# Unused columns that move the operand tiles of TensorE to other offsets within 512 bytes

## The chip, the core and the metric

The kernel runs on one core of one Trainium2 chip. Its time is the device time of one launch in microseconds (us): 2973.36 us, the median of three runs (2969.99 to 2975.42). The execution that was profiled took 2971.34 us.

## The reference

Two token streams of 256 tokens each and width 1024, a context (columns 0 to 255 of every tile below) and a latent one (columns 256 to 511), go through four layers. Every layer has a token mixer and then a SwiGLU feed-forward network (FFN); both read an RMSNorm of the stream that is scaled and shifted by vectors made from `c` or `c_ctx`. Layers 0 and 3 mix with a bidirectional state-space scan (SSD), layer 1 with a gated MLP (gMLP), layer 2 with bidirectional retention. The last layer computes the latent stream alone.

```
for i in range(4):
    x = x + g1 * mixer[i % 3](modulate(rmsnorm(x, norm1_g[i]), sh1, sc1))        # latent reads context through scan states
    x = x + g2 * (silu(h @ ffn_w1[i]) * (h @ ffn_w3[i])) @ ffn_w2[i]             # h = modulate(rmsnorm(x, norm2_g[i]), sh2, sc2)
    (the context stream likewise, with its own shifts, scales and gates, except in the last layer)
return rmsnorm(x, final_g)
```

Nearly all of the arithmetic is in the dense products with the weights: `ssd_w_in`, `ssd_w_out`, `gmlp_w_in`, `gmlp_w_out`, `ret_w_in`, `ret_w_out`, and the FFN's three, 1024 by 2816 and back.

## The kernel before

Everything is held with the features on the 128 partitions and the tokens along the free axis. A product of float32 accuracy is made of three float32r products: a matrix is split into a high part (rounded to float32r) and a low part (what the rounding left), and high times high, high times low and low times high are added up in PSUM (`mm3`, L302 to L308). So each pair of 128x128 weight block and activation block gives three matmuls, each with a load of its own for its 128x128 stationary operand:

```
            pe.matmul(pt, lh, rh, start=(start and i == 0), stop=False)
            pe.matmul(pt, lh, rl, start=False, stop=False)
            pe.matmul(pt, ll, rh, start=False, stop=(stop and i == n - 1))
```

The first two arguments behind `pt` are the stationary operand and the moving one; the trace prints the moving one first (`mm<-AH,whi`: `AH` moves, `whi` is stationary). L306 is the first of the three, L307 the second, L308 the third. There are 4,304 of each.

The weights stream in through `emit_dma` and `emit_split`: 512 KB units on SyncE's queue into three staging tiles `st`, split by ScalarE into `whi` (L226) and by VectorE, every fourth time GpSimd, into `wlo` (L227), four buffers of each. Splitting runs three units ahead of the product that uses them.

The moving operands are: `AH`/`AL`, the split normed stream (`proj`, used by all input products); `yg` (from `ytiles`), the split gated output of the mixers and the last four inner tiles of each FFN; in the gMLP for every other block `yh`/`yl`; in the FFN `hh`/`hl` (made by `pair`, two inner tiles of 512 tokens in each, six buffers of each), which `oblock` multiplies with `ffn_w2`. In `wide_job` (gMLP and retention values) it is the other way around: the weights move and `AH`/`AL` are stationary. With both streams a moving operand is 512 columns of float32 (2,048 bytes in each partition), in the last layer and where a stage is started stream by stream it is 256.

Where stages meet, splits that are ahead are put into tiles of the next stage that are free until then (`place`): `hh`/`hl` of the FFN, `V` of the gMLP, `dcc`/`dcl` of the retention, `C2`/`px` of the SSD. They then are stationary operands under those names.

The order of the instructions on each engine is the order in which the program is written out (`tc.manual_schedule`): lists of jobs and slots, with the number of splits ahead as the only rule. Tiles come from pools. A pool takes the next free bytes of a partition's row; a tile is placed behind the one that was first asked for before it, rounded up to 32 bytes, and tiles with a `tag` share `bufs` buffers. The constants' pool `cp` lies first, from byte 16,512 (after the scratch and four constants); `X`, `AH` and `AL` are its first three tiles. `MHALF`, 4 columns with the exponent -0.5 for the norms, stands behind them; after it come `SEL`, `CC`, `IDB`, `NEG0`, `NEG1` and the `yg` tiles, then the pools `wp` (`st`, `whi`, `wlo`) and `sp`, and last the pool of the running stage (`ssd`, `gml`, `ret`, `ffn`, `mod`).

Of the kernel before, what the change touches and what calls it, by code (L numbers as in the profile page):

```python
# [9 lines left out]
F32 = mybir.dt.float32  # L10
F32R = mybir.dt.float32r
# [5 lines left out]
P = 128  # L17
# [3 lines left out]
NTOK = 2 * T  # L21
# [7 lines left out]
FFN_START = (0, 6, 12, 18)  # L29
STOP = DEPTH  # L30
POOL_SHARE = 4


_PRM = {}
# [77 lines left out]
def backbone(ctx, tc, A, out):  # L112
# [3 lines left out]
    cp = ctx.enter_context(tc.tile_pool(name="cp", bufs=1))  # L116
# [6 lines left out]
    def nm(s):  # L123
        serial[0] += 1
        return f"{s}_{serial[0]}"
# [3 lines left out]
    def psum_open(ph, **split):  # L129

        assert sum(split.values()) == 8
        banks["pool"] = ph.enter_context(tc.tile_pool(name=nm("pp"), bufs=1, space=PSUM))
        banks["split"] = split
        banks["cycle"] = [0, ["mm"]]
# [4 lines left out]
    def psm():  # L139
        c = banks["cycle"]  # L140
        c[0] += 1
        return ps(c[1][c[0] % len(c[1])])
# [4 lines left out]
    def f32(ap):  # L147
        return ap.bitcast(F32)
# [6 lines left out]
    CST = cp.tile([P, NCST], F32, name="CST")  # L155
    MOD = cp.tile([P, DEPTH, 2, 48], F32, name="MOD")
    GP = cp.tile([P, DEPTH, 2, 2, 8], F32, name="GP")
    MHALF = cp.tile([P, 4], F32, name="MHALF")
    SEL = cp.tile([P, 64], F32R, name="SEL")
    CC = cp.tile([P, KT, 32], F32, name="CC")  # L160
    BF = mybir.dt.bfloat16
# [22 lines left out]
    lent = set()  # L184
    share = [POOL_SHARE]
    hold = [False]
# [115 lines left out]
    def mm3(pt, pairs, start=True, stop=True):  # L302

        n = len(pairs)
        for i, (lh, ll, rh, rl) in enumerate(pairs):
# [3 lines that stand above are left out]
# [10 lines left out]
    def mjob(unit, evac, n0=0, n1=NTOK):  # L319
        def q(W):  # L320
            evac(proj(W[0], n0, n1), n0, n1)
        return Job([unit], [(q, [0], [0])])

    def mjob_skew(units, evacs, ranges, whole=True):


        quanta = []
        n0, n1 = ranges[0][0], ranges[-1][1]
        pts = {}

        def half(j, a, b, h):
            def f(W):
                if j not in pts:
                    pts[j] = psm()[:, :n1 - n0]
                hi, lo = W[j]
                mm3(pts[j][:, a - n0:b - n0], [
                    (hi[:, k * P:(k + 1) * P], lo[:, k * P:(k + 1) * P], AH[:, k, a:b], AL[:, k, a:b])
                    for k in range(4 * h, 4 * h + 4)], start=(h == 0), stop=(h == 1))
                if h == 1 and not whole:
                    evacs[j](pts.pop(j)[:, a - n0:b - n0], a, b)  # L340
                elif h == 1 and b == n1:
                    evacs[j](pts[j], n0, n1)
            return f
        for a, b in ranges:
            for j in range(0, len(units), 2):
                for h in range(2):
                    for jj in range(j, min(j + 2, len(units))):
                        quanta.append((half(jj, a, b, h), [jj], [jj] if h == 1 and b == n1 else []))
        return Job(units, quanta)
# [122 lines left out]
    def rms_steps(acc, n0, n1, dim, sink):  # L472
# [5 lines left out]
        def s0():  # L478
# [8 lines left out]
            dve.tensor_scalar(ms[:, :nch], pt[:, :nch], 1.0 / dim, EPS, op0=MUL, op1=ADD)  # L487
            pool.tensor_tensor(st["rs"][:, :nch], ms[:, :nch], MHALF[:, :nch], op=POW)

# [84 lines left out]
    def ytiles():  # L574

        return [[cp.tile([P, NTOK], F32R, tag=f"y{a}{k}", name=nm("yg"), bufs=1) for k in range(4)]
                for a in "hl"]


    def resid(i, w, norm):  # L580
        def f(pt, m, n0, n1, last):
            for a, b in split_ranges(n0, n1):
                g = MOD[:, i, vec(a), 24 * w + 16 + m:24 * w + 16 + m + 1]
                dve.scalar_tensor_tensor(  # L584
                    X[:, m, a:b], pt[:, a - n0:b - n0], g, X[:, m, a:b], op0=MUL, op1=ADD)
                if last and (a in norm):
                    norm[a].add(m, dve if m >= 5 + (i < 3 or w == 1) and a == T else pool)
        return f
# [29 lines left out]
    def boundary(last, norms, nxt, ranges, hooks=None, lend=(), pool_share=1):  # L618
# [39 lines left out]
        for k, q in enumerate(open_job(nxt) if nxt is not None else []):  # L658
# [7 lines left out]
            if k == 7:  # L666
                share[0] = POOL_SHARE
        share[0] = POOL_SHARE
        banks["cycle"][1] = ["mm"]
# [558 lines left out]
    def gmlp(i, j, need_ctx, prev_last, prev_ranges, norms, fin_norms):  # L1228
        UN, VN, WOUT = Src("gmlp_u", j), Src("gmlp_v", j), Src("gmlp_out", j)
        with ExitStack() as ph:  # L1230
# [24 lines left out]
            def vnorm():  # L1255
                t = qt([4], "vn")
                dve.tensor_reduce(t, SS, axis=mybir.AxisListType.X, op=ADD)
                dve.tensor_scalar(t, t, 1.0 / 2048.0, EPS, op0=MUL, op1=ADD)
                pool.tensor_tensor(RS, t, MHALF, op=POW)

# [258 lines left out]
    def ffn(i, need_ctx, prev_last, prev_ranges, norms, fin_norms):  # L1519
        W1, W3, W2A, W2B = Src("ffn_w1", i), Src("ffn_w3", i), Src("ffn_w2a", i), Src("ffn_w2b", i)  # L1520
        yr = BOTH if need_ctx else LAT
        n0, n1 = yr[0][0], NTOK
        with ExitStack() as ph:
            q = ph.enter_context(tc.tile_pool(name=nm("ffn"), bufs=1))
            psum_open(ph, mm=7, s=1)
            H = {}
            S1 = {}

            def e1(ct):
                def f(pt, a, b):  # L1530
                    t = q.tile([P, NTOK], F32, tag="s1", name=nm("s1"), bufs=2)
                    act.activation(t[:, :b - a], pt, AF.Silu)  # L1532
                    S1[ct, a] = t
                return f

            def pair():
                return [q.tile([P, 2, NTOK], F32R, tag=t, name=nm(t), bufs=6) for t in ("hh", "hl")]

            def place():
                return [t.rearrange("p a b -> p (a b)") for t in pair()]  # L1540

            def e3(ct):
                def f(pt, a, b):
                    s = S1.pop((ct, a))[:, :b - a]
                    dve.tensor_tensor(s, s, pt, op=MUL)  # L1545
                    if ct == 18 and ct not in H:
                        yt = ytiles()
                        for k in range(4):
                            H[18 + k] = (yt[0][k], yt[1][k])
                    elif ct not in H:  # L1550
                        hh, hl = pair()
                        for k in range(2):
                            H[ct + k] = (hh[:, k], hl[:, k])
                    hh, hl = H[ct]
                    act.copy(hh[:, a:b], s)  # L1555
                    dve.tensor_tensor(hl[:, a:b], s, f32(hh[:, a:b]), op=SUB)
                return f

            def hid(ct):
                return [mjob(W1[ct], e1(ct), n0, n1), mjob(W3[ct], e3(ct), n0, n1)]  # L1560

            ev = resid(i, 1, fin_norms)

            def oblock(kb):
                nk, k0 = FFN_BLOCKS[kb], FFN_START[kb]

                def lazy(m):
                    def q_(W):
                        hi, lo = W[0]
                        pt = psm()[:, :n1 - n0]  # L1570
                        mm3(pt, [(hi[:, k * P:(k + 1) * P], lo[:, k * P:(k + 1) * P],
                                  H[k0 + k][0][:, n0:n1], H[k0 + k][1][:, n0:n1]) for k in range(nk)])
                        ev(pt, m, n0, n1, False)
                    return Job([W2A[kb, m]], [(q_, [0], [0])], 0.75)
                return [lazy(m) for m in range(KT)]

            first_job = mjob_skew([W1[0], W3[0], W1[1], W3[1]], [e1(0), e3(0), e1(1), e3(1)], yr)
            boundary(prev_last, norms, first_job, prev_ranges,
                     lend=[place, place] if need_ctx else [], pool_share=1 if 0 < i < 3 else 2)
            if i == 0 or i + 1 < STOP:  # L1580
                mod_open(ph)
            bg = mod_steps(i + 1, 0, 48) if i + 1 < STOP else []
            seq = []
            for ct in range(2, 12):
                seq += hid(ct)
            seq += oblock(0)
            for ct in range(12, 18):
                seq += hid(ct)
            seq += oblock(1)
            for ct in range(18, 22):  # L1590
                seq += hid(ct)
            seq += oblock(2)
            if i == 0:

                bg = mod_steps(0, 40, 48) + bg
                if STOP == 1:
                    run(seq[:16], bg)
                    seq, bg = seq[16:], []
            run(seq, bg, tail=0)

            k0 = FFN_START[3]
            last = out_last([W2B[mp_] for mp_ in range(4)],
                            lambda: [[H[k0 + k][a] for k in range(4)] for a in range(2)], ev, yr)
            return last, yr
# [8 lines left out]
    act.activation(CC, CC, AF.Silu)  # L1613
    pool.memset(MHALF, -0.5)

# [243 lines left out]
```

## Time and profile before

| | |
|---|---|
| median of three runs | 2973.36 us |
| the profiled execution | 2971.34 us, of which 2969.5 us from its first to its last instruction (the span) |
| TensorE matmul busy | 96% of the span, 16,132 matmuls |
| TensorE weight load busy | 81% |
| VectorE, ScalarE, GpSimd busy | 65%, 37%, 18% |
| DMA engines | 376.37 MB, mean 127 GB/s |
| mean granted TensorE clock | 0.987 of full speed |

PE is TensorE's matmul, PEld its weight load, DVE VectorE, ACT ScalarE, POOL GpSimd. Matmuls are pipelined: the duration of one (0.40 us for 512 columns) overlaps that of the next, so what a matmul costs in a stream is the distance from its start to the start of the next. The timeline view gives the starts: over a run of matmuls that follow each other without a wait, the last start less the first, over the number of steps, is the cost of one.

### The profile page before, as it was taken

How to read it: one execution, taken by the hardware profiler on the slowest of the kernel's cores; microseconds unless marked ns; L12 is line 12 of the kernel's file. 1: busy time of each engine (PE TensorE's matmuls, PEld its weight loads, DVE VectorE, ACT ScalarE, POOL GpSimd, SP SyncE). 2: the span in 40 equal slices, each digit the busy share in tenths (PEclk: the TensorE clock that was granted, in tenths of full speed). 3: DMA queues.
4: the chain of work that ended last, by engine and by line, in shares of the span. 5: the costliest groups of instructions: out<-in, count | busy, mean ns of one | idle time of the engine just before them, and what ended most of it. 6: DMA issues, size and time to landing. Idle time of an engine off the chain costs nothing. (4 is left out here: it accounts for less than half of the span.)

```text
span 2969.5 us, 40647 instructions
## 1 busy us (share of the span) xinstructions
PE 2863.9 (96%) x16132; PEld 2394.7 (81%) x16132; DVE 1923.8 (65%) x3049; ACT 1097.2 (37%) x1934; POOL 529.1 (18%) x405
## 2 busy tenths in 40 slices
PE   7999999899999999999999999999999999999898
PEld 4777777788889878888888777778888888888898
DVE  5776767687875165577776334346777778787644
ACT  4455444322224422422224322234222245544443
POOL 1211112211112100211112111112111142112222
PEclk9999999899999999999999999999999999999899
DMA  6222233255553222355443222223554422223454
GB/s 232 101 86 100 86 107 114 91 189 196 186 183 107 92 78 92 105 183 176 169 169 114 71 74 82 80 77 109 184 183 170 163 86 93 84 87 111 142 178 140
DMA packets 111678, 376.37 MB, mean 127 GB/s; under 512 B 12160, under 2 KB 16640, under 8 KB 111488
## 3 DMA queue, kind: packets, MB, share of 16 engines
q1 hardware_dynamic: 109296, 367.23, 35.6%
q0 software_dynamic: 1616, 5.77, 0.6%
q8 instruction: 127, 2.08, 0.3%
q10 hardware_dynamic: 576, 0.77, 0.1%
q14 instruction: 63, 0.52, 0.1%
HBM read 369.53 MB, written 4.19 MB: 126 GB/s over the span
## 5 line engine op out<-in xcount | busy, mean ns | idle before, releaser
L306 PE MATMUL mm<-AH,whi 128*128 128x512 f32 (+1 forms) x2456 | 897.3, 365 | 4.4 <-DVE xs L823 1.6
L307 PE MATMUL mm<-AL,whi 128*128 128x512 f32 (+1 forms) x2456 | 887.9, 362 | 0.0
L308 PE MATMUL mm<-AH,wlo 128*128 128x512 f32 (+1 forms) x2456 | 886.8, 361 | 0.0
L226 ACT CAST whi<-st 128x1024 fp32r<-128x1024 f32 (+1 forms) x502 | 504.0, 1007 | 362.0 <-PE mm L307 223.8
L227 DVE TENSOR_TENSOR wlo<-st,whi 128x1024 fp32r<-128x1024 f32 (+1 forms) x372 | 448.6, 1210 | 263.5 <-ACT whi L226 263.2
L227 POOL TENSOR_TENSOR wlo<-st,whi 128x1024 fp32r<-128x1024 f32 (+1 forms) x130 | 325.8, 2506 | 1524.9 <-ACT whi L226 1520.3
L306 PEld LDWEIGHTS mm<-AH,whi 128*128 128x128 f32 x2456 | 465.0, 189 | 88.1 <-issue 7.1
L308 PEld LDWEIGHTS mm<-AH,wlo 128*128 128x128 f32 x2456 | 464.6, 189 | 77.8
L307 PEld LDWEIGHTS mm<-AL,whi 128*128 128x128 f32 x2456 | 464.8, 189 | 77.1 <-issue 1.2
L412 DVE SCALAR_TENSOR_TENSOR mj<-mst,cb 128x1024 bf16<-128x1024 f32 x304 | 440.9, 1450 | 34.4 <-DMA mst<-in_mod_w_dram 28.4
L584 DVE SCALAR_TENSOR_TENSOR X<-mm,MOD,X 128x256 f32<-128x256 f32 x332 | 148.1, 478 | 145.8 <-PE mm L308 145.2
L306 PE MATMUL mm<-yg,whi 128*128 128x256 f32 (+1 forms) x592 | 200.2, 338 | 18.7 <-DVE X L584 5.3
L308 PE MATMUL mm<-hh,wlo 128*128 128x512 f32 (+1 forms) x576 | 210.9, 366 | 0.0
L307 PE MATMUL mm<-hl,whi 128*128 128x512 f32 (+1 forms) x576 | 210.8, 366 | 0.0
L306 PE MATMUL mm<-hh,whi 128*128 128x512 f32 (+1 forms) x576 | 210.8, 366 | 0.0
L307 PE MATMUL mm<-yg,whi 128*128 128x256 f32 (+1 forms) x592 | 192.6, 325 | 1.3 <-DVE yg L1089 1.0
L308 PE MATMUL mm<-yg,wlo 128*128 128x256 f32 (+1 forms) x592 | 192.4, 325 | 0.0
L1555 ACT CAST hh<-s 128x512 fp32r<-128x512 f32 (+1 forms) x72 | 40.9, 567 | 297.6 <-DVE s L1545 297.6
L1545 DVE TENSOR_TENSOR s<-s,mm 128x512 f32<-128x512 f32 (+1 forms) x88 | 54.6, 620 | 147.3 <-PE mm L308 147.3
L306 PEld LDWEIGHTS mm<-yg,whi 128*128 128x128 f32 x592 | 113.4, 191 | 33.6 <-DVE X L1133 5.4
L1532 ACT ACTIVATE s<-mm 128x512 f32<-128x512 f32 (+1 forms) x88 | 47.9, 544 | 216.6 <-PE mm L308 216.5
L307 PEld LDWEIGHTS mm<-hl,whi 128*128 128x128 f32 x576 | 108.3, 188 | 19.8
(362 smaller groups left out, 4056.8 us busy)
## 6 DMA issues: line engine op xcount, KB each, us to landing
st<-in_ffn_w_dram SPq DMA_DIRECT2D x176, 512.0 KB, 3.3
mst<-in_mod_w_dram SPq DMA_DIRECT2D x152, 512.0 KB, 4.2
st<-in_ssd_in_dram SPq DMA_DIRECT2D x82, 512.0 KB, 3.3
st<-in_ffn_w2a_dram SPq DMA_DIRECT2D x96, 384.0 KB, 3.0
st<-in_ssd_out_dram SPq DMA_DIRECT2D x32, 512.0 KB, 3.3
st<-in_ret_in_dram SPq DMA_DIRECT2D x32, 512.0 KB, 3.3
st<-in_mod_n_dram SPq DMA_DIRECT2D x24, 512.0 KB, 4.0
st<-in_ffn_w2b_dram SPq DMA_DIRECT2D x16, 512.0 KB, 3.3
```

Source lines behind the costliest of these rows:

```text
L226: act.copy(hi[:, :n], t[:, :n])
L227: (pool if i % share[0] == 0 else dve).tensor_tensor(lo[:, :n], t[:, :n], f32(hi[:, :n]), op=SUB)
L306: pe.matmul(pt, lh, rh, start=(start and i == 0), stop=False)
L307: pe.matmul(pt, lh, rl, start=False, stop=False)
L308: pe.matmul(pt, ll, rh, start=False, stop=(stop and i == n - 1))
L412: dve.scalar_tensor_tensor(j, t, 1.0, mp[1][:, v], op0=MUL, op1=MUL, accum_out=MOD[:, i, v, ct:ct + 1])
L584: dve.scalar_tensor_tensor(X[:, m, a:b], pt[:, a - n0:b - n0], g, X[:, m, a:b], op0=MUL, op1=ADD)
L1532: act.activation(t[:, :b - a], pt, AF.Silu)
L1545: dve.tensor_tensor(s, s, pt, op=MUL)
L1555: act.copy(hh[:, a:b], s)
```

## The change

Three pieces of never-read columns are put in. `MHALF` is asked for with 28 columns in place of 4, and its first four are used: what lies behind it moves by 96 bytes. In each FFN, the first time that `pair` makes its two tiles, a pad of 48 columns (192 bytes) is put before the first `hh` and one of 32 columns (128 bytes) between the `hh` and the `hl` buffers.

```
+PAD_W, PAD_H = 24, (48, 32)
...
-    MHALF = cp.tile([P, 4], F32, name="MHALF")
+    MHALF = cp.tile([P, 4 + PAD_W], F32, name="MHALF")[:, :4]
...
+            pads = []
...
             def pair():
-                return [q.tile([P, 2, NTOK], F32R, tag=t, name=nm(t), bufs=6) for t in ("hh", "hl")]
+                r = []
+                for t, n in zip(("hh", "hl"), PAD_H):
+                    if len(pads) < 2:
+                        pads.append(q.tile([P, n], F32, name=nm("pad")))
+                    r.append(q.tile([P, 2, NTOK], F32R, tag=t, name=nm(t), bufs=6))
+                return r
```

The instructions and their order on every engine stay the same; what changes is where tiles lie. Every tile of the table is a multiple of 512 bytes long, and so are the blocks that the products take out of it, so that a tile has one offset within 512 bytes, whichever buffer and block is used:

| tile | offset modulo 512 before | after |
|---|---|---|
| `X`, `AH`, `AL` | 128 | 128 |
| `st`, `whi`, `wlo`, `yg` | 480 | 64 |
| `hh` | 160 | 448 |
| `hl` | 160 | 64 |
| `V` of the gMLP | 256 | 352 |
| `yh`, `yl` of the gMLP | 288 | 384 |
| `dcc`, `dcl` of the retention | 192 | 288 |
| `C2`, `px`, `E` and the rest of the SSD's large tiles | 480 | 64 |

From this follows, for each kind of product, the distance from the stationary operand's offset to the moving one's (moving less stationary, modulo 512):

| moving / stationary | columns | distance before | after |
|---|---|---|---|
| `AH`, `AL` / `whi`, `wlo` | 512 and 256 | 160 | 64 |
| `hh` / `whi`, `wlo` | 512 and 256 | 192 | 384 |
| `hl` / `whi` | 512 and 256 | 192 | 0 |
| `yg` / `whi`, `wlo` | 512 and 256 | 0 | 0 |
| `yh`, `yl` / `whi`, `wlo` | 512 | 320 | 320 |
| `whi`, `wlo` / `AH`, `AL` | 512 | 352 | 448 |
| `AH`, `AL` / `hh`, `hl` | 256 | 480 | 192, 64 |
| `AH`, `AL` / `dcc`, `dcl` | 256 | 448 | 352 |

## Rows read from the trace of the kernel before

**Rows 1.** The page, busy time and share of the span by engine.
```profile
PE 2863.9 (96%) x16132; PEld 2394.7 (81%) x16132; DVE 1923.8 (65%) x3049; ACT 1097.2 (37%) x1934; POOL 529.1 (18%) x405
```

**Rows 2.** Busy us by stretch (windows): PE, PEld, DVE, ACT, POOL; clock, DMA.
```profile
1190.00:1570.00 380.00, 377.00 (x1803) 311.45 (x1804) 271.84 (x400) 112.09 (x156) 61.25 (x39) 1.00 0.46 161
2384.00:2722.00 338.00, 318.14 (x2419) 287.21 (x2419) 269.73 (x477) 169.18 (x362) 86.64 (x92) 0.98 0.25 88
```

**Rows 3.** Groups by line and shape, xcount, busy us, mean ns, idle before.
```profile
L306 PE MATMUL mm<-AH,whi 128*128 128x512 f32 x1696 | 679.5, 401 | 1.6 <-DVE xs L823 1.6
...
L306 PE MATMUL mm<-AH,whi 128*128 128x256 f32 x760 | 217.8, 287 | 2.7 <-ACT AH L566 1.1 <-DVE GP L442 1.0 <-DVE X L1133 0.6
...
L306 PE MATMUL mm<-hh,whi 128*128 128x512 f32 x432 | 170.6, 395 | 0.0
...
L306 PE MATMUL mm<-whi,AH 128*128 128x512 f32 x256 | 101.9, 398 | 0.0
```

**Rows 4.** Timeline, PE, `AH`/`AL` by weights, 512 columns: start us, us.
```profile
601.77 0.40 PE L308 MATMUL mm<-AH,wlo 128*128 128x512 f32 x1
...
625.91 0.39 PE L306 MATMUL mm<-AH,whi 128*128 128x512 f32 x1
```

**Rows 5.** Timeline, PE, `hh`/`hl` by weights, 512 columns.
```profile
783.19 0.39 PE L306 MATMUL mm<-hh,whi 128*128 128x512 f32 x1
...
803.95 0.39 PE L308 MATMUL mm<-hh,wlo 128*128 128x512 f32 x1
```

**Rows 6.** Timeline, PE, `yg` by weights, 512 columns.
```profile
1128.49 0.39 PE L307 MATMUL mm<-yg,whi 128*128 128x512 f32 x1
...
1135.29 0.39 PE L307 MATMUL mm<-yg,whi 128*128 128x512 f32 x1
```

**Rows 7.** Timeline, PE, gMLP `yh`/`yl` by weights, 512 columns.
```profile
1081.18 0.39 PE L307 MATMUL mm<-yl,whi 128*128 128x512 f32 x1
...
1087.36 0.39 PE L307 MATMUL mm<-yl,whi 128*128 128x512 f32 x1
```

**Rows 8.** Timeline, PE, weights by `AH`/`AL` (`wide_job`), 512 columns.
```profile
970.82 0.39 PE L308 MATMUL mm<-whi,AL 128*128 128x512 f32 x1
...
998.82 0.39 PE L308 MATMUL mm<-whi,AL 128*128 128x512 f32 x1
```

**Rows 9.** Timeline, PE, 256 columns, `AH`/`AL` by weights, last FFN.
```profile
2799.78 0.28 PE L308 MATMUL mm<-AH,wlo 128*128 128x256 f32 x1
...
2814.92 0.28 PE L308 MATMUL mm<-AH,wlo 128*128 128x256 f32 x1
```

**Rows 10.** Timeline, PE, 256 columns, `hh`/`hl` by weights, last FFN, first block.
```profile
2836.74 0.28 PE L308 MATMUL mm<-hh,wlo 128*128 128x256 f32 x1
...
2849.94 0.28 PE L306 MATMUL mm<-hh,whi 128*128 128x256 f32 x1
```

**Rows 11.** Timeline, PE, 256 columns, `hh`/`hl` by weights, last FFN, third block.
```profile
2929.75 0.28 PE L308 MATMUL mm<-hh,wlo 128*128 128x256 f32 x1
...
2941.99 0.28 PE L308 MATMUL mm<-hh,wlo 128*128 128x256 f32 x1
```

**Rows 12.** Timeline, PE, 256 columns, `AH`/`AL` by `dcc`/`dcl`, start of the retention.
```profile
1594.28 0.28 PE L306 MATMUL g<-AH,dcc 128*128 128x256 f32 x1
...
1596.66 0.28 PE L306 MATMUL g<-AH,dcl 128*128 128x256 f32 x1
```

**Rows 13.** Timeline, PE, 256 columns, the same operands, next pair of jobs.
```profile
1599.78 0.28 PE L307 MATMUL g<-AL,dcc 128*128 128x256 f32 x1
...
1600.96 0.28 PE L308 MATMUL g<-AH,dcl 128*128 128x256 f32 x1
```

**Rows 14.** Timeline, PE, 256 columns, `yg` by weights.
```profile
1191.08 0.28 PE L306 MATMUL mm<-yg,whi 128*128 128x256 f32 x1
...
1204.15 0.28 PE L307 MATMUL mm<-yg,whi 128*128 128x256 f32 x1
```

**Rows 15.** Groups by line and shape: the weight load of the first product.
```profile
L306 PEld LDWEIGHTS mm<-AH,whi 128*128 128x128 f32 x2456 | 465.0, 189 | 88.1 <-issue 7.1 <-ACT whi L226 2.2 <-ACT AH L566 1.8
```

## Prediction

> **What bounds the kernel.** I read the page's busy shares first: PE is busy for 2863.9 of 2969.5 us, 96%, and the next engine, DVE, for 65% [rows 1]. Then the busy time by stretch, since a mean over stages can hide one with another limit: in the second FFN PE works 377.0 of 380 us and DVE 271.8, and even in the last SSD, the stage with the most small work, PE has 318 of 338 us against 270 for DVE and 169 for ACT [rows 2]; the granted clock there is 1.00 and 0.98, the level of 2.4 GHz nearly throughout. So PE sets the pace in every stage, and a matmul that gets cheaper or dearer moves the end almost one for one. Last I read the timeline, because the groups' mean durations (0.40 us for 512 columns) overlap and don't give the cost of a matmul. Its starts do: in long runs without a wait, cost is the distance from start to start.
>
> These distances are the core of the case, since all runs below have the same three instructions and the same number of columns:
>
> - `AH`/`AL` by weights, 512 columns, operands 160 bytes apart: 103 steps in 625.91 - 601.77 = 24.14 us, 234.4 ns each [rows 4].
> - `hh`/`hl` by weights, 192 apart: 89 steps in 20.76 us, 233.3 ns [rows 5].
> - weights by `AH`/`AL`, 352 apart: 120 steps in 28.00 us, 233.3 ns [rows 8].
> - `yh`/`yl` by weights, 320 apart: 27 steps in 6.18 us, 228.9 ns [rows 7].
> - `yg` by weights, 0 apart: 30 steps in 6.80 us, 226.7 ns [rows 6].
>
> 512 columns at 2.4 GHz are 213.3 ns, so each pays 13 to 21 ns on top. With 256 columns (106.7 ns): `AH` by weights 129 steps in 15.14 us, 117.4 ns [rows 9]; `yg` 109 steps in 13.07 us, 119.9 ns [rows 14]; `hh` 117.9 ns in one block (112 steps, 13.20 us) [rows 10] and 113.3 ns in a later one on the same buffers and offsets (108 steps, 12.24 us) [rows 11]; `AH` by `dcc`/`dcl` 113.3 ns (21 steps, 2.38 us) [rows 12] and 118.0 ns (10 steps, 1.18 us) [rows 13]. Buffers, PSUM banks and blocks change all along these runs and the distance does not; what differs between the groups is which tiles are read, and so their offsets.
>
> Here a rule speaks against the change. The Trainium skill, "SBUF — State Buffer", section "Who interferes with whom", says that TensorE has one read port for the moving operand and another for LDWEIGHTS, independent of each other, and never waits for anyone. By it the offsets could not matter and the sum of this change would be zero; the 7.7 ns between [rows 4] and [rows 6] are not explained by it.
>
> **What the change does, part by part.** No instruction is added, removed or moved on any engine or queue, and no wait. The pads cost bytes of SBUF alone. What changes is the distance between the two operands that TensorE reads at once: the load of the next stationary operand takes 189 ns [rows 15] and so lies beside the running matmul.
>
> *`AH`/`AL` by weights, 160 to 64.* L306 has 1,696 such matmuls with 512 columns [rows 3], times three lines 5,088. No row has a distance of 64. Two pairs of rows tell which is its nearest: distances 192 (`hh`) and 448 (`dcc`), 256 apart, show the same two values with 256 columns, about 118 and 113.3 ns [rows 10 to 13], while their neighbours show others. I read this as a pattern that repeats after 256 bytes; then 64 is like 320, which is `yh` with 228.9 ns [rows 7]. From 234.4 to 228.9 is 5.5 ns, times 5,088 makes 28.0 us saved. Bounds: at best the 226.7 ns of `yg`, 7.7 ns, 39.2 us saved; on the other side nothing measured lies above 234.4, so I allow as much above it as the best row lies below: 39.2 us lost.
>
> *`hh`/`hl` by weights, 192 to 384 and 0.* 3 x 432 = 1,296 matmuls with 512 columns [rows 3]. A third of them, with `hl`, goes to distance 0: 226.7 ns. For 384 no row with 512 columns exists; between the extremes 226.7 and 234.4 I take the middle, 230.5. The mean (2 x 230.5 + 226.7) / 3 = 229.3 is 4.0 ns under the 233.3 of now: 5.2 us saved. Bounds 8.6 us saved (all at 226.7), 8.6 lost by the same mirror.
>
> *Weights by `AH`/`AL`, 352 to 448.* 3 x 256 = 768 matmuls [rows 3]. If the pattern repeats after 256, 448 is like 192, 233.3 ns as now [rows 5, 8]: 0. Bounds 5.1 us saved or lost (6.6 ns each).
>
> *256 columns.* `AH` by weights, 3 x 760 = 2,280 [rows 3], 160 to 64: rows span 113.3 to 119.9 around 117.4 [rows 9 to 14], and one pair of offsets takes two values, so I take 0, bounds 9.3 us saved (4.1 ns), 9.3 lost.
>
> *What stays:* `yg` and `yh`/`yl` keep their distances, 0 and 320: nothing. The float32 products, DVE, ACT, POOL and the DMAs read and write the same lengths: nothing.
>
> Sum: 28.0 + 5.2 = 33.2 us less. Bounds: all savings 39.2 + 8.6 + 5.1 + 9.3 = 62 us, all losses the same. What could take a gain back is another engine: in the second FFN 380 us would become some 372, with DVE's 272 still far below [rows 2]; ACT and POOL have more room. So I let all of it through. The profiled execution took 2971.34 us, 2.0 under the median of three, 2973.36; against the median the forecast is 2973.4 - 33.2 = 2940 us.
>
> **Rivals.**
>
> *1. The distance 64 is worse (slower).* The place is the 5,088 matmuls of `AH`. The weight load and the moving read both run up their rows while a matmul lasts, and at 64 bytes one may keep meeting the other for longer than at 160. Its price goes up to the mirror bound, 39.2 us on `AH` less the 5.2 of `hh`: 3007 us; with half of the price, 19.6 - 5.2 = 14.4 us, it is 2988. It decides once the step of `AH` is over 235.4 ns (1 ns more is 5.1 us, what `hh` gives). For it: five distances give no smooth curve, so a sixth can lie anywhere. Against: `AH` is already the slowest of the five.
>
> *2. Offsets don't matter (no change).* The difference between [rows 4] and [rows 6] would come from where tiles lie in the large, or from what is stored, and moving them by 96 bytes leaves the steps as they are: 2973 us, within 3. For it: two values for the same offsets [rows 10, 11], which an offset alone can't explain. Against: with 512 columns each kind keeps its step in every buffer, `hh` and `hl` over twelve buffers across 49 KB. This is the result that the Trainium skill's page "SBUF — State Buffer" leads to.
>
> *3. All kinds reach the best row (much faster).* 64, 384 and 448 are all as good as 0, and 256 columns fall to 113.3 ns: 62 us less, 2911; with a lower step than any row shows (for 512 columns as little on top as the 6.6 ns of 113.3 over 106.7, that is 220 ns) it would be 14.4 x 5,088 = 73 us for `AH` alone, 2900 without the rest. For it: the 6.6 ns show that less than 13 ns on top is possible. Against: no run of 512 columns comes below 226.7.
>
> *4. PE gets faster and the end doesn't.* A stage would have to be bound elsewhere. [rows 1, 2] speak against it everywhere; I give it no case of its own, it shades the forecast to 2950 at most.
>
> **How the numbers follow.** About 0.2%, 6 us, is what a measurement of this kernel can tell from no change. The forecast, `AH` at 227 to 233 ns, 10 to 50 us less: 0.55. Rival 3: 0.15. Rival 2, with gains or losses of under 6 us from any mixture: 0.12. Rival 1: 0.18. Faster is then 0.55 + 0.15 = 0.70, same 0.12, slower 0.18. The likeliest case alone spans 2923 to 2963. For 8 in 10 the range takes in most of rival 3, down to 2900, and rival 2 and the lighter half of rival 1, up to 2985.
>
> **What would show it.** In the timeline of the changed kernel: the step of `AH` by `whi` with 512 columns in a long run of an FFN (229 by the forecast, 234.4 by rival 2, over 235.4 by rival 1, 227 or less by rival 3); the step of `hh`/`hl` (229, or 233.3); that of `yg` unchanged at 226.7 and of `yh` at 228.9, the proof that distance and not the offset itself counts; that of the weights by `AH` at 233.3. Wrong would be the whole picture if `yg` changed its step though its distance stays 0, or if the steps fell and the span did not. The idle times of PE, the groups of DVE and ACT and the DMAs should stay as they are.

## The result

The changed kernel takes 2939.23 us (median of four runs, 2937.81 to 2940.90) against 2973.45 before: a ratio of 0.9889, 95% interval 0.9875 to 0.9903, so 34 us or 1.1% faster. The forecast was 2940. The profiled execution took 2938.11 us with a span of 2936.3, 33.2 us under the span of before, at the same mean granted clock (0.989 and 0.987).

### The profile page after: what moved, and what is told of

Same layout as the page of the kernel before. It is cut to its first block, busy times and chain, and to the rows that moved or that the text cites. A ratio compares the mean times of both kernels' runs of the same rounds, so it can differ in the third digit from the quotient of the medians.

```text
span 2936.3 us, 40649 instructions
## 1 busy us (share of the span) xinstructions
PE 2830.9 (96%) x16132; PEld 2389.1 (81%) x16132; DVE 1927.5 (66%) x3049; ACT 1096.1 (37%) x1934; POOL 525.5 (18%) x405
## 5 line engine op out<-in xcount | busy, mean ns | idle before, releaser
L308 PE MATMUL mm<-AH,whi 128*128 128x512 f32 (+1 forms) x2456 | 886.9, 361 | 4.4 <-DVE xs L825 1.6
L308 PEld LDWEIGHTS mm<-AH,whi 128*128 128x128 f32 x2456 | 463.9, 189 | 82.1 <-issue 6.9
L308 PE MATMUL mm<-yg,whi 128*128 128x256 f32 (+1 forms) x592 | 199.3, 337 | 17.8 <-DVE X L1135 4.8
L308 PE MATMUL mm<-hh,whi 128*128 128x512 f32 (+1 forms) x576 | 210.7, 366 | 0.0
L308 PEld LDWEIGHTS mm<-yg,whi 128*128 128x128 f32 x592 | 112.4, 190 | 32.7 <-issue 6.1
L310 PEld LDWEIGHTS mm<-hh,wlo 128*128 128x128 f32 x576 | 107.9, 187 | 19.0
```

## The profile after

The page's busy time by engine, as in [rows 1], and the same two windows as in [rows 2] (PE, PEld, DVE, ACT, POOL; clock, DMA share, GB/s):

```profile
PE 2830.9 (96%) x16132; PEld 2389.1 (81%) x16132; DVE 1927.5 (66%) x3049; ACT 1096.1 (37%) x1934; POOL 525.5 (18%) x405
```
```profile
1190.00:1570.00 380.00, 376.93 (x1866) 317.52 (x1865) 276.23 (x411) 114.66 (x162) 64.13 (x45) 1.00 0.48 166
2384.00:2722.00 338.00, 309.92 (x2408) 279.61 (x2406) 276.16 (x487) 167.60 (x358) 86.89 (x88) 0.98 0.28 96
```

The counts of the page are those of before, instruction for instruction, and PE's busy time is 33.0 us shorter, all of the gain. The other engines work as long as they did, within 4 us. The windows are the same in clock time, so they hold other work now and their counts don't compare; what they show is that PE still works 376.9 of 380 us there, with DVE at 276.

The groups by shape, beside those of [rows 3] (mean ns of one behind the comma; the two lines that the change adds shift L306 to L308):

```profile
L308 PE MATMUL mm<-AH,whi 128*128 128x512 f32 x1696 | 670.9, 396 | 1.6 <-DVE xs L825 1.6
...
L308 PE MATMUL mm<-AH,whi 128*128 128x256 f32 x760 | 216.1, 284 | 2.8 <-ACT AH L568 1.1 <-DVE GP L444 1.0 <-DVE X L1135 0.6
...
L308 PE MATMUL mm<-hh,whi 128*128 128x512 f32 x432 | 169.8, 393 | 0.0
...
L308 PE MATMUL mm<-whi,AH 128*128 128x512 f32 x256 | 101.4, 396 | 0.0
```

Idle time before these lines is what it was, 1.6, 2.8 (2.7 before), 0.0 and 0.0 us. Only the matmuls themselves are shorter: 5 ns for `AH`, 2 for `hh` in this line. How much a matmul costs the timeline tells (start us, duration us); its starts answer to rows 4 to 9:

```profile
566.18 0.39 PE L309 MATMUL mm<-AL,whi 128*128 128x512 f32 x1
...
673.99 0.39 PE L309 MATMUL mm<-AL,whi 128*128 128x512 f32 x1
675.13 0.39 PE L308 MATMUL mm<-hh,whi 128*128 128x512 f32 x1
...
705.80 0.39 PE L310 MATMUL mm<-hh,wlo 128*128 128x512 f32 x1
...
1118.85 0.39 PE L310 MATMUL mm<-yg,wlo 128*128 128x512 f32 x1
...
1125.88 0.39 PE L308 MATMUL mm<-yg,whi 128*128 128x512 f32 x1
...
1062.20 0.39 PE L310 MATMUL mm<-yh,wlo 128*128 128x512 f32 x1
...
1068.84 0.39 PE L309 MATMUL mm<-yl,whi 128*128 128x512 f32 x1
...
940.53 0.39 PE L308 MATMUL mm<-whi,AH 128*128 128x512 f32 x1
...
968.53 0.39 PE L308 MATMUL mm<-whi,AH 128*128 128x512 f32 x1
...
2838.09 0.28 PE L309 MATMUL mm<-AL,whi 128*128 128x256 f32 x1
...
2851.99 0.28 PE L310 MATMUL mm<-AH,wlo 128*128 128x256 f32 x1
```

| product, columns | rows before | distance | step before, ns | distance | step after, ns |
|---|---|---|---|---|---|
| `AH`/`AL` by weights, 512 | [rows 4] | 160 | 234.4 | 64 | 107.81 us over 471 steps: 228.9 |
| `hh`/`hl` by weights, 512 | [rows 5] | 192 | 233.3 | 384, 0 | 30.67 over 134: 228.9 |
| `yg` by weights, 512 | [rows 6] | 0 | 226.7 | 0 | 7.03 over 31: 226.8 |
| `yh`/`yl` by weights, 512 | [rows 7] | 320 | 228.9 | 320 | 6.64 over 29: 229.0 |
| weights by `AH`/`AL`, 512 | [rows 8] | 352 | 233.3 | 448 | 28.00 over 120: 233.3 |
| `AH`/`AL` by weights, 256 | [rows 9] | 160 | 117.4 | 64 | 13.90 over 118: 117.8 |

This is the picture that the forecast asked for. `yg` and `yh` moved by 96 bytes together with the weights and kept their steps; the two whose distance changed, and was forecast to matter, changed.

## Experiments

In each, a step is again the start of a matmul to the start of the next. Means over a whole kernel take the steps without a wait and leave out those over 250 ns (150 with 256 columns), which are 84 of 5,223 before and 100 after for `AH` by weights with 512 columns. Each of the three kernels of matmuls alone ran once.

### The two parts alone

The first moves the weights and all that lies behind them by 96 bytes and leaves `hh` and `hl` without pads; the second has the pads in the FFN alone.

```
-PAD_W, PAD_H = 24, (48, 32)
+PAD_W, PAD_H = 24, (0, 0)       # w_only; and the pad only where n > 0
+PAD_W, PAD_H = 0, (48, 32)      # h_only
```

> Only the 24 columns behind MHALF: split weights and gated tiles at 64, hh and hl both at 256, so their distance to the weights stays 192. Theory (the distance between the two operands, modulo 256, sets the step of a matmul): AH by whi with 512 columns 229.0 ns a step, hh and hl 233.3 as before, time about 27 us under before, 2946. Rival (the pads of the FFN do it, or the two parts only work together): AH stays at 234.3 and the time at 2973.

> Only the two pads of the FFN: hh at 352, hl at 480, weights at 480 as before, so the distances are 384 and 0 as in the changed kernel, and AH by whi keeps 160. Theory: AH 234.3 ns a step, the run of hh, hl, hh 228.9 on average (as in the changed kernel), time 5 to 6 us under before, 2968. Rival (offsets that are multiples of 64 bytes matter, not the distance): hh and hl stay at 233.3, the time at 2973.

`w_only` took 2945.12 us against 2971.3 of before on the same chip, ratio 0.9907 (0.9893 to 0.9922); `h_only` 2966.26, ratio 0.9982 (0.9973 to 0.9990). The timeline of `w_only`, first `AH`, then `hh`/`hl`, which lie 192 bytes from the weights again:

```profile
567.08 0.39 PE L308 MATMUL mm<-AH,whi 128*128 128x512 f32 x1
...
674.89 0.39 PE L308 MATMUL mm<-AH,whi 128*128 128x512 f32 x1
...
677.19 0.40 PE L309 MATMUL mm<-hl,whi 128*128 128x512 f32 x1
...
709.15 0.39 PE L308 MATMUL mm<-hh,whi 128*128 128x512 f32 x1
```

`AH` has 228.9 ns (107.81 us over 471 steps) as in the whole change; `hh`/`hl` have 233.3 (31.96 us over 137) as before, though they lie 96 bytes further on. In `h_only` it is the other way around: `AH` stays at 234.2 ns in the mean over the kernel, and `hh`/`hl` fall to 228.9 (31.59 us over 138), in the mean over the kernel `hh` to 230.4 and `hl` to 226.0:

```profile
683.11 0.39 PE L309 MATMUL mm<-hl,whi 128*128 128x512 f32 x1
...
714.70 0.39 PE L309 MATMUL mm<-hl,whi 128*128 128x512 f32 x1
```

The savings, 26.2 and 5.0 us, add up to 31.2, the change's 34 within what the runs vary.

### The same distances elsewhere

The kernel before with 24 unused columns ahead of `X`: every tile lies 96 bytes further on, every distance stays.

```
+    cp.tile([P, 24], F32, name="padx")
     X = cp.tile(...)
```

> The kernel before with one pad of 24 columns ahead of X: every tile moves by 96 bytes, AH to 224, weights and yg to 64, hh and hl to 256; all distances are those of before. Theory: steps as before (AH 234.3, hh 233.3, yg 226.7 with 512 columns), time 2973. Rival (the offset of the weights, or of all tiles, relative to 64 or 512 bytes matters by itself): AH falls towards 229 as in the changed kernel, the time to 2940 to 2946.

It took 2968.82 us, ratio 0.9995 (0.9987 to 1.0004): no change. `AH` by weights:

```profile
570.20 0.40 PE L309 MATMUL mm<-AH,wlo 128*128 128x512 f32 x1
...
681.26 0.39 PE L309 MATMUL mm<-AH,wlo 128*128 128x512 f32 x1
```

That is 111.06 us over 474 steps, 234.3 ns, as slow as in [rows 4]. So it is not the weights' own offset that made `AH` faster in the change: it is 64 here too.

### 256 bytes more

The changed kernel with 88 columns behind `MHALF` in place of 24: `AH` by weights goes from a distance of 64 to 320, weights by `AH` from 448 to 192.

```
-PAD_W, PAD_H = 24, (48, 32)
+PAD_W, PAD_H = 88, (48, 32)
```

> The changed kernel with 64 columns more behind MHALF: weights and yg at 320, hh 192, hl 320; the distance of AH to the weights is 320 in place of 64, that of the weights to AH 192 in place of 448, the others as in the changed kernel. Theory with a pattern of 256 bytes: AH 229.0 ns, weights by AH 233.3, time as the changed kernel, 2939. Rival (a pattern of 512 bytes): the step of AH is another one, anything from 220 to 242, the time off by 5 us for each ns.

It took 2938.12 us, ratio 0.9886 (0.9873 to 0.9899) against the change's 0.9889.

```profile
566.27 0.39 PE L310 MATMUL mm<-AH,wlo 128*128 128x512 f32 x1
...
674.07 0.39 PE L310 MATMUL mm<-AH,wlo 128*128 128x512 f32 x1
```

107.80 us over 471 steps, 228.9 ns: 64 and 320 are alike here, the guess on which the forecast rested.

### Matmuls alone, one distance after the other

A kernel that computes nothing of the reference: it loads 8 KB per partition, copies it into a moving tile `M` and a stationary tile `W`, and runs 48 matmuls at each distance.

```
        o = (at + d) // 4
        for k in range(N):                          # N = 48; w is W, src is M
            m = o + 512 * (k % 3 if cols == 512 else k % 4)
            b = at // 4 + 128 * (k % 5)
            pe.matmul(pt[:rows, :cols], w[:, b:b + rows], src[:, m:m + cols], start=(k == 0), stop=(k == N - 1))
```

> Nothing of the reference is computed: matmuls alone, in runs of 48 with a weight load each, moving operand M and stationary W both at offset 128, M read from d bytes further on. Runs wa to wp: 512 columns, d = 0 to 240 in steps of 16; ha to hp the same with 256 columns, ra to rp once more in the other direction; v and g: d = 256 to 480 in steps of 32; na, ne, nk: d = 0, 64, 160 with 64 stationary columns. Theory (distance modulo 256): 512 columns 226.7 ns at 0, 229 at 64, 233.3 at 96 and 192, 234.3 at 160, and each v as the w at d - 256; 256 columns 120 at 0, 117.8 or 113.3 at 64 and 192. If the weight load is what costs, half a load (64 columns) takes the step nearer to 213 ns. Rival (other engines' traffic at SBUF, which here is all but gone, makes the excess): all runs alike, near 216 ns.

Timeline, grouped by run (start us, us, xcount): the start of one run to the start of the next, over 48, is the step. `wa` has distance 0, `we` 64, `wk` 160, `wp` 240:

```profile
22.01 11.04 PE L39 MATMUL wa<-M,W 128*128 128x512 f32 x48
32.89 11.28 PE L39 MATMUL wb<-M,W 128*128 128x512 f32 x48
...
66.40 11.16 PE L39 MATMUL we<-M,W 128*128 128x512 f32 x48
77.40 11.25 PE L39 MATMUL wf<-M,W 128*128 128x512 f32 x48
...
133.14 11.41 PE L39 MATMUL wk<-M,W 128*128 128x512 f32 x48
144.39 11.36 PE L39 MATMUL wl<-M,W 128*128 128x512 f32 x48
...
189.23 11.05 PE L39 MATMUL wp<-M,W 128*128 128x512 f32 x48
200.12 5.91 PE L39 MATMUL ha<-M,W 128*128 128x256 f32 x48
```

10.88 / 48 = 226.7 ns, 11.00 / 48 = 229.2, 11.25 / 48 = 234.4, 10.89 / 48 = 226.9: the kernel's own steps, with next to nothing at work beside PE: from 20 to 554 us VectorE is busy for 15.2 us (it copies 64 columns of each run), ScalarE and GpSimd not at all, and the DMA engines for 1%. That ends the rival that the traffic of the other engines is part of it. Over the last 33 steps of each run all sixteen distances from 0 to 240 lie between 226.7 and 234.6 ns, and the eight that were run 256 bytes further on agree with theirs within 0.9. Columns 256 give 113.3 to 120.0, without the same order: 0 is the best at 512 columns and at 256, with 80 and 96, the slowest of the sixteen. Nor do 256 columns keep to one value. Run once more in the other direction, four of the sixteen (16, 32, 128 and 144) came out 1.1 to 2.1 ns away, and of the eight pairs that are 256 bytes apart three differ by more than 1 ns, most of all 192 and 448 with 113.4 and 117.8. One expectation missed: with 64 stationary columns in place of 128, the steps were 230.0, 228.3 and 233.5 ns at 0, 64 and 160. Half a weight load doesn't halve what is paid over 213.3.

### Two better layouts, and the change again

From these steps two layouts follow that should beat the change. `all_zero` puts `AH`, the weights, `yg`, `hh` and `hl` all at offset 128; `ah_minus_16` puts `AH` and `AL` 16 bytes below the others, a distance of 240, whose step alone was as good as that of 0 at 512 columns and better at 256 (117.2 for 120.0).

```
-PAD_W, PAD_H = 24, (48, 32)
+PAD_W, PAD_H = 40, (80, 0)      # all_zero; and a pad only ahead of hh
+PAD_W, PAD_H = 48, (80, 0)      # ah_minus_16; the same, and:
+    AH = cp.tile([P, KT * NTOK + 64], F32R, name="AH")[:, 4:4 + KT * NTOK].rearrange("p (k n) -> p k n", k=KT)
+    AL = cp.tile([P, KT * NTOK + 64], F32R, name="AL")[:, 4:4 + KT * NTOK].rearrange("p (k n) -> p k n", k=KT)
```

> The changed kernel with other pads: 40 columns behind MHALF and 80 before hh, none between hh and hl, so that AH, the weights, yg, hh and hl all lie at offset 128 and the distance is 0 in every dense product but yh's. By the distance theory and the steps measured so far: AH at 512 columns 226.7 ns in place of 229.2 (5,123 x 2.5 = 12.7 us less), hh 226.7 for 230.4 (861 x 3.7 = 3.2 us less), weights by AH 226.7 for 233.4 (767 x 6.7 = 5.1 us less), AH at 256 columns 120.0 for 117.3 (2,336 x 2.7 = 6.4 us more): 14.6 us under the changed kernel, some 2924 us. Rival, the steps have a floor near 229 ns for AH because the other engines write beside it: some 2935 us, with AH staying at 229.

> The changed kernel with the weights, yg, hh and hl at one offset modulo 256 and AH and AL 16 bytes below it (16 unused columns of AH's and AL's tiles put their data at 144, the others lie at 160): distance 240 for AH by weights, 0 for yg, hh and hl, 16 for weights by AH. By the distance theory with the steps of the matmuls that ran alone: AH at 512 columns 226.7 for 229.2 (12.7 us less), at 256 columns 117.2 for 117.3 (0), hh 226.7 for 230.4 (3.2 us less), weights by AH 231.5 for 233.4 (1.5 us less): 17.4 us under the changed kernel, some 2922 us, the fastest so far. Rival, that only tiles on a multiple of 64 bytes read well: AH at 144 is on none, its step is then no better than 229.2 and the time no better than 2935 us.

> The changed kernel once more, on the same chip as the other kernels of this call, to compare them with: 2939 us by every theory.

On one chip, against 2968.84 us of before: the change 2939.53, ratio 0.9902 (0.9890 to 0.9915); `all_zero` 2925.47, ratio 0.9862 (0.9849 to 0.9875), the fastest of all; `ah_minus_16` 2959.79, ratio 0.9963 (0.9950 to 0.9977), 38 us over its expectation. `AH` by weights in `all_zero`, with 512 and with 256 columns:

```profile
564.13 0.39 PE L308 MATMUL mm<-AH,whi 128*128 128x512 f32 x1
...
670.89 0.39 PE L308 MATMUL mm<-AH,whi 128*128 128x512 f32 x1
...
2806.07 0.28 PE L310 MATMUL mm<-AH,wlo 128*128 128x256 f32 x1
...
2839.19 0.28 PE L310 MATMUL mm<-AH,wlo 128*128 128x256 f32 x1
```

226.7 ns (106.76 us over 471 steps) and 120.0 (33.12 us over 276), both as in the matmuls alone, and the sum of terms, 14.6 us under the change, came out as 14.1. In `ah_minus_16`:

```profile
572.03 0.40 PE L310 MATMUL mm<-AH,wlo 128*128 128x512 f32 x1
...
679.95 0.40 PE L310 MATMUL mm<-AH,wlo 128*128 128x512 f32 x1
```

107.92 us over 456 steps, 236.7 ns, where 226.7 was expected; 235.0 in the mean over 5,124 steps. That is 8.3 x 5,124 = 43 us, more than the whole miss. The rival of the 64-byte multiples had foreseen it, with a step no better than 229.2 and a time no better than 2935; the next two kernels tell whether for the right reason. Weights by `AH`, 16 bytes apart, came out better than alone, 226.9 for 231.5 ns (3.5 us over 767 steps). `hh` at 0 (226.7) and `AH` with 256 columns (117.2) were as expected.

### Finer distances, lengths and types

The same matmuls alone, at other distances, lengths and types.

```
+            run(pre + L[j], cols, 212 + 4 * j)       # j = 0 to 15; pre is "w" with 512 columns, "h" with 256
...
+        run("o" + L[j], 512, (0, 64, 160, 240)[j], at=32)
+        run("q" + L[j], 256, (0, 64, 160, 240)[j], at=32)
...
+        run("t" + L[j], 384, (0, 64, 160)[j])        # and bfloat16: bb, bc, bd
```

> Matmuls alone once more, runs of 48, nothing of the reference computed: distances 212 to 272 in steps of 4 bytes with 512 and with 256 columns; distances 0, 64, 160 and 240 with both operands 32 bytes further on; 384 columns at 0, 64 and 160; and bfloat16 operands. If the step is set by which 16-byte piece of a 256-byte line the operands start in, it stays the same over four distances of 4 bytes and jumps between them; if by the bytes themselves, it changes with each. With both operands 32 bytes further on nothing changes if the distance alone counts (226.7, 228.9, 234.3, 226.7 ns at 512 columns); if each offset counts, at least one is off by over 2 ns. At 384 columns (160 ns at full speed) the excess at distance 0 is 13 ns if it is paid once per matmul as at 256 and 512 columns, 10 if it goes by the columns.

Distance 240 took 236.6 ns here with the stationary operand where it was in the first run, and 226.7 with both 32 bytes further on. Two values at one distance: this is where the expectation of `ah_minus_16` went wrong, and the rival of the 64-byte multiples doesn't hold either, since neither run at 226.7 had its moving operand on one. Distance 64 took 233.3 with both 32 bytes further on, behind a run of 256 columns (`ob`, 11.20 us over 48):

```profile
310.03 11.37 PE L45 MATMUL ob<-M,W 128*128 128x512 f32 x48
321.23 5.82 PE L45 MATMUL qb<-M,W 128*128 128x256 f32 x48
```

By the test of the expectation, one step off by over 2 ns, each offset would count by itself. The last kernel takes this back: there 64 takes 228.9 ns twice with both 32 bytes further on. Steps of 4 bytes change the result each time (212 to 228: 239.2, 233.3, 231.1, 233.3, 235.6 ns), so it does not go by 16-byte pieces. Then the lengths and types (`tb`, `tc`: 384 columns at 64 and 160; `bb` and `bc`: bfloat16 at 0 and 80):

```profile
368.61 8.48 PE L45 MATMUL tb<-M,W 128*128 128x384 f32 x48
376.93 8.49 PE L45 MATMUL tc<-M,W 128*128 128x384 f32 x48
385.26 10.53 PE L45 MATMUL bb<-MB,WB 128*128 128x512 bf16 x47
395.63 10.52 PE L45 MATMUL bc<-MB,WB 128*128 128x512 bf16 x47
```

With 384 columns the step is 173.3 ns at 64 as at 160 (8.32 us over 48), 13.3 over the 160 ns of the columns, and 173.3 at 0 too: of these three distances none makes a difference. In bfloat16 the pair of rows shows 48 matmuls in 10.37 us (one is missing from the trace), 216.0 ns, and 215.8 over the steady steps at both distances: 2.5 ns over the columns. This agrees with the formula of the Trainium skill, "TensorE: Matmul & The Clock Gate", section "Back-to-back issue gap" (columns by 2.4 GHz plus 2.5 ns). That section of the Trainium skill gives the formula for a matmul by itself and some 131 ns at 512 columns for a stream of loads and matmuls; this is such a stream, and 215.8 is what it took. The float32r products stay 4 ns (256 columns) to 11 ns (512) above the formula at best, 113.3 and 226.7. It is not the type alone that differs: the bfloat16 loads are recorded with 97 ns, those of float32r with 188.

### What ran before

The last kernel puts the same distances behind different ones, in several PSUM banks, with both operands 32 bytes further on, behind a pause, and with each weight block loaded twice in a row as the products of the kernel do.

```
+    runs("a", (0, 240, 64, 240, 0, 64, 160, 64, 236, 240))   # aa to aj; in groups of their own:
+    runs("b", (0, 240, 64, 160, 64), at=32)
+    runs("c", (240,) * 6)
+    runs("d", (240, 240, 240, 64, 64, 64, 160, 0), pause=True)
+    runs("e", (0, 240, 64, 240), triple=True)
+    runs("f", (16, 0, 16, 48, 16))
```

> Matmuls alone, 512 columns, runs of 48, nothing of the reference computed. The same distances come behind different ones, in six PSUM banks, with both operands 32 bytes further on, behind a pause in which ScalarE rewrites the weights, and with each weight block loaded twice in a row as in the kernel. Distance 240 took 226.7 ns in one run of matmuls and 236.6 in another, at the same offsets. If what ran before decides which of two patterns is kept, 240 takes 226.7 ns behind 0 and about 236 behind 236, and six runs of 240 in a row keep one value; behind a pause all starts are alike and 240 takes one value each time. If the PSUM bank decides, the six in a row differ and repeat. If the loads' order decides, the runs with blocks loaded twice take about 235, as in the kernel with AH 16 bytes lower. Distance 0 takes 226.7 in all of these by every theory, distance 160 about 234; 64 takes 228.9 or 233.3.

```profile
21.77 11.36 PE L47 MATMUL ab<-M,W 128*128 128x512 f32 x48
32.97 11.17 PE L47 MATMUL ac<-M,W 128*128 128x512 f32 x48
43.97 11.50 PE L47 MATMUL ad<-M,W 128*128 128x512 f32 x48
55.31 11.07 PE L47 MATMUL ae<-M,W 128*128 128x512 f32 x48
```

`ab` and `ad` have the same distance, 240, the same tiles and the same code. Behind a run at 0, `ab` takes 11.20 us (233.3 ns a step); behind a run at 64, `ad` takes 11.34 (236.2, steady 236.7). Six runs of 240 in a row, in six banks, keep 236.6; behind a pause the first takes 233.3 and the next two 236.8. With each block loaded twice the values are the same, 233.3 behind 0 and 236.7 behind 64. With the 226.7 of the earlier runs that makes three steady values for one distance, and without a pause they go by what ran before: 233.3 three times out of three behind 0, 236.6 or 236.7 three times out of three behind 64. Of the expectation the bank and the order of the loads fall, and the exact values missed (behind 0 it isn't 226.7). Behind a pause they missed too: the first two runs there both come behind 240 and still keep two values, so the distance of the run before isn't all that counts. Distances 0, 64 and 160 took 226.7, 228.9 and 234.1 ns in every place they had in this kernel but the very first, in 5, 9 and 3 runs, behind a pause or not. Distance 16 kept 231.6 to 231.8 behind 240, 0 and 48, so the 226.9 that weights by `AH` took at 16 in `ah_minus_16` is a second value too.

The trace of `ah_minus_16` holds all three values of 240 by itself. `AH` by weights, 512 columns, early in the first layer, and behind `hh`/`hl` (distance 0) in the first FFN:

```profile
62.48 0.39 PE L308 MATMUL mm<-AH,whi 128*128 128x512 f32 x1
...
85.38 0.39 PE L310 MATMUL mm<-AH,wlo 128*128 128x512 f32 x1
...
717.09 0.40 PE L308 MATMUL mm<-AH,whi 128*128 128x512 f32 x1
...
784.06 0.40 PE L310 MATMUL mm<-AH,wlo 128*128 128x512 f32 x1
```

That is 226.7 ns (22.90 us over 101 steps), with `AH` at 144 and thus on no multiple of 64, and 233.3 (66.97 over 287). Six long stretches come behind `hh`/`hl`, and all six keep 233.3, as behind 0 in the matmuls alone; the three that come behind `AH` with 256 columns keep 236.7. In the changed kernel all thirteen stretches of 70 steps or more end at 228.9. The sums that held, in the change and in `all_zero`, rest on 0, 64 and 320; the one that failed rests on 240.

## Why the prediction was right

**PE bounds every stage.** Right: matmuls shortened by some 33 us, and the span by 33.2, with the idle times of PE (84.4 us in all before, 84.1 after) and the groups of the other engines as they were. No engine gave anything back. The clock gave back some 2.4 us: behind four waits for `V` in the gMLP the granted clock fell to half, the level of 1.2 GHz, and twelve matmuls of `AH` took 5.21 us in place of 2.75 (the columns are those of [rows 2]):

```profile
1033.40:1040.20 6.80, 6.32 (x16) 4.96 (x17) 4.93 (x9) 1.57 (x2) 0.00 (x0) 0.50 0.00 0
```

Before, the same waits at 1041 to 1046 us left it at 1.00. The traces of all the other kernels that compute the reference show the fall, `all_by_96` with its old distances too, so it doesn't come of the distances.

**Offsets matter by the distance between the operands.** Right for 512 columns, and shown apart from its rivals: moving all tiles together changed nothing (0.9995), moving the weights by 96 bytes against `AH` gave 26 us. The distance doesn't settle the step by itself, as 240 shows. The rule of the Trainium skill, "SBUF — State Buffer", section "Who interferes with whom", by which TensorE's two reads are independent and never wait, does not hold for these float32r products in the sense that would have counted here: the step of the same matmul lies anywhere from 226.7 to 239.2 ns by the operands' place. What it is inside TensorE that takes longer no run showed.

**The pattern repeats after 256 bytes.** Right where it was used, 64 like 320 and 448 like 192, and with 512 columns within 0.9 ns at eight distances alone. What it was read from was weaker than it looked: that 192 and 448 share the two values 118 and 113.3 with 256 columns says little, since 64 shows 113.3 and 117.8 as well, and alone 192 and 448 differ by 4.4 ns. With 512 columns no two of its rows were 256 apart; `w_plus_256` bore the guess out afterwards. It was lucky in one thing more: 64 has a second value, 233.3, seen once alone. Had `AH` kept that one, it would have saved 1 ns a matmul and the change some 10 us.

**The terms.** Each product's count, times the difference of its mean steps over the whole of both traces:

| term | forecast, us | measured, us |
|---|---|---|
| `AH` by weights, 512 | -28.0 | 5,088 x (234.2 - 229.2) = -25.6 |
| `hh`/`hl` by weights, 512 | -5.2 | 1,296 x (233.3 - 228.9) = -5.7 |
| weights by `AH`, 512 | 0 | 768 x (233.4 - 233.3): 0 |
| `AH` by weights, 256 | 0 | 2,280 x (118.1 - 117.3) = -2.0 |
| `hh`/`hl` by weights, 256 | 0 | 432 x (116.3 - 119.8) = +1.5 |
| `AH` by `hh`/`hl`, 256 | none | 288 x (118.3 - 114.7) = -1.0 |
| sum | -33.2 | -32.8, of 33.2 in the span |

`AH` was sized too high by 2.4 us: over the whole traces the means are 234.2 and 229.2 where the long runs had 234.4 and 228.9, and the difference shrinks from 5.5 to 5.0 ns. After the change the first steps of a run cost more than the rest (230.3 ns in the first seven of each run), before it they did not (233.8). The middle taken for `hh` at 384, 230.5 ns, was a guess between two ends and met 230.4 (alone, 384 took 233.5; here two matmuls in three have it and the third has 0); `hl` at 0 took 226.0 for 226.7. With 256 columns the terms are small and of both signs, as their 0 had it. That the sum came out so exactly is in part luck: these errors cancel. So do the steps that the means leave out. With every step counted from start to start, waits and the slow clock included, `AH` with 512 columns gave 22.3 us, `hh`/`hl` 5.7, `AH` and `yg` with 256 columns 2.6 and 1.6, and everything else 1.2.

**The rivals.** A distance of 64 that is worse than 160 didn't come, but `ah_minus_16` shows that the case was real: a step of 235.0 exists in this kernel, at a distance that looked best elsewhere. No change is ruled out by the interval. All kinds at the best row (2911 us) would have needed 64, 384 and 448 to be as good as 0; none of the three is. `all_zero`, which has 0 in place of all three, comes to 2925, mainly since the products of 256 columns then take 120.0 ns and not the 113.3 of that rival.

## What to carry to other kernels

Where TensorE bounds a kernel of float32r products, read the step from start to start per pair of tiles; groups that differ with the same columns are worth a look at where their operands lie modulo 256 bytes, and a few unused columns are all it takes to move them. Take a distance that shows one value behind all kinds of predecessors (here 0, at 226.7 ns for 512 columns), not the best value of one run. Weigh 256 columns apart from 512: the distance that was best for one was among the slowest for the other.

## What was not expected of the hardware

One distance can have several steady steps. Distance 240 kept 226.7, 233.3 or 236.7 ns over whole runs of matmuls, and without a pause the run before went with the value. With 256 columns this shows in the changed kernel itself:

```profile
559.83 0.28 PE L308 MATMUL mm<-AH,whi 128*128 128x256 f32 x1
...
564.93 0.28 PE L308 MATMUL mm<-AH,whi 128*128 128x256 f32 x1
```

45 steps in 5.10 us, 113.3 ns, for the same product and the same offsets that take 117.8 in the last FFN; so do the 117.9 and 113.3 of [rows 10, 11]. Some steady steps are the columns' time and a multiple of 6.67 ns (16 cycles at 2.4 GHz) on top: 13.3 ns (twice) at distance 0 with 256, 384 and 512 columns and 20 (three times) at 192 with 512. Others are not, such as 15.6 at 64 and 21.0 at 160, so this is no rule. Of the two types tried, float32r pays this and bfloat16 had 2.5 ns. Which step follows from a distance and a predecessor stays open; the runs give a table, not a law. It also stays open why 384 columns show one value at the three distances tried.
